# Second block's attention: three distances of the head planner and the spacing in the last group are changed

## Chip, core and metric

The kernel runs on one core of one Trainium2 chip. The metric is the device time of one execution in microseconds (us); the time of before is the median of three runs. Engines are called as the profile calls them: PE (TensorE, matmuls), DVE (VectorE), ACT (ScalarE), POOL (GpSimd) and SP (SyncE, which here only issues DMAs). PEld is PE's weight load.

## What is computed

Two transformer blocks follow each other on 256 tokens of width 2048, all in fp32. The first block (a gated delta rule, an RWKV scan, cross attention, an MLP) is not touched. The second block projects to q, k, v and a gate g for 32 heads of width 64. Sixteen heads (groups (0,0) and (0,1), eight heads each) mix three dilated windows, and sixteen (groups (1,0) and (1,1)) attend in a 2-D neighbourhood. Both come down to a softmax over at most 256 keys with a bias that also carries the mask:

```python
s = einsum('bhqd,bhkd->bhqk', q, k) * scale + bias
p = softmax(s)
o = einsum('bhqk,bhkd->bhqd', p, v)
y = concat(o) * silu(g)
out = layer_norm(ALPHA * x + y @ w_out)
```

## The kernel before

Each fp32 product is made of three matmuls over halves hi and lo: hi*hi, lo*hi, hi*lo. A weight matrix comes in pieces of 512 KB (`piece`, line 132): SP fetches `raw`, ACT rounds it to `whi` (line 106), DVE takes the rest, `wlo` = raw - whi (line 143). raw, whi and wlo have three buffers each. One piece feeds 12 matmuls of 128x512 (in `as_parts`, used for v) or 24 of 128x256 (in `ws_parts`, used for q, k and g). These matmuls write `acc` and are called big products below.

In the second block `main2` yields the big products of v, q and k for one group of eight heads, then for the next, and at last the gates of group (0,0) and (0,1). A group's heads are handed over when its k is complete; they run beside the big products that come next. So the heads of (0,0), (0,1) and (1,0) run beside v, q and k of the group after them, and those of (1,1) beside two gates. Heads are numbered 0 to 31 here in that order: 0 to 7 are the first group, 24 to 31 the last.

A head (`head`, from line 1374) has three places on PE, and yields twice between them:

- S, the scores: four matmuls into `s2p`. Then DVE adds the bias and takes the maximum (L1395, two of them, and L113), ACT takes the exponential with its sum (`s` on L106, two of them), DVE inverts the sum (L1401) and scales (L115, two of them).
- T, the transposition: four matmuls of `s` into `t2p` (L196). Then ACT rounds it to `ph`, and DVE takes the rest, `pl`.
- O, the output: four matmuls `o2p` from v, `ph` and `pl`. Then ACT and DVE add the two halves into `oall`.

PE's order is written by hand. `steps` keeps a count `now` that grows by 0.66 for each few big products and by the first number of a head's yield; the second number is how far `now` has to move on before the head's next place may be issued. `HEADS` (8.0) and `HEADS_END` (5.5, last group) are the distances between the starts of two heads, and the 7.0 in the loop is the distance between the end of a group's k and its first head. `main2` yields None before k of a group is written out, and then all heads that still run are finished first. DVE, ACT, POOL and SP are ordered by the tile framework's scheduler, which sees PE's order; `whi` and `wlo` have high priority there. Each engine works its own list in order. The PSUM buffers of s2p, t2p and o2p are four in one ring; `bias`, `s`, `ph` and `pl` have three buffers each. A head's bias is fetched by SP two heads ahead (`ta` for the first two groups, `tn` for the last two, where POOL adds a mask), and may start once L1395 of the head three before it is done. SP's list holds these fetches between the fetches of weights.

Of the kernel before, what the change touches and what calls it, by code (L numbers as in the profile page):

```python
# [19 lines left out]
ALPHA = 2.0 ** 0.25  # L20
C_DECAY = 0.5 * math.exp(-0.5)
INV_LAT = 42.0
HEADS, HEADS_END = 8.0, 5.5
WARM = 11
PART = 0.66

# [39 lines left out]
def block_kernel(tc, a, out, dbg=None, stop=99):  # L66
# [35 lines left out]
    def mm(o, l, r, start=True, stop=True):  # L102
        nc.tensor.matmul(o, l, r, start=start, stop=stop)  # L103

    def act(o, i, f=AF.Copy, **kw):
        return nc.scalar.activation(o, i, f, **kw)  # L106

    def tt(o, x, y, op, eng=None):
        (eng or nc.vector).tensor_tensor(out=o, in0=x, in1=y, op=op)  # L109

    def ts(o, x, s1, op0, s2=None, op1=None, eng=None):
        if op1 is None:
            (eng or nc.vector).tensor_scalar(out=o, in0=x, scalar1=s1, scalar2=None, op0=op0)  # L113
        else:
            (eng or nc.vector).tensor_scalar(out=o, in0=x, scalar1=s1, scalar2=s2, op0=op0, op1=op1)  # L115
# [6 lines left out]
    def pst(shape, name):  # L122
        return PS["pool"].tile(shape, F32, name=name, tag="ps", bufs=8 - PS["mm"])
# [70 lines left out]
    def tr(o, i):  # L194
        n = i.shape[0]
        nc.tensor.transpose(o, i, ident[0:n, 0:n])  # L196
# [45 lines left out]
    def split(src, h, l, scale=None):  # L242

        if scale is None:
            act(h, src)
            tt(l, src, h.bitcast(F32), SUB)
        else:
            act(h, src, scale=scale)
            stt(l, src, scale, h.bitcast(F32), MUL, SUB)
# [828 lines left out]
    now, need, ms = 0.0, None, main()  # L1078
    with tc.manual_schedule(engines={nc.tensor.engine}):
        while True:  # L1080
# [6 lines left out]
            if q is not None:  # L1087
                if stage[q][3] not in done:
                    stage[q][1] = now + 0.1
                    r = 0, 0.1  # L1090
                else:
                    r = next(stage[q][0], "end")
# [12 lines left out]
            if need is None and ms is not None:  # L1105
                r = next(ms, "end")
# [8 lines left out]
            else:  # L1115
                now = max(now, min(u[1] for u in stage if u and not u[2]))
# [180 lines left out]
    def at2(shape, name, bufs=1, dt=F32):  # L1297
        return atp.tile(shape, dt, name=name, tag=name, bufs=bufs)
# [78 lines left out]
    def head(key, i, bias):  # L1377

        c, e = divmod(i, 2)
        grp, hf = key  # L1380
        if not bias:
            bias[:] = [(bias_a, bias_b)[grp](8 * hf + j) for j in range(2)]
        q, (k, kl) = qk["q", c, key], qk["k", c, key]
        b = bias.pop(0)
        sp = pst([128, 2, T], "s2p")
        for t in range(2):
            tk = slice(t * 128, t * 128 + 128)
            mm(sp[:, t, :], q[:, e, tk], k[:, e, :], stop=False)
            mm(sp[:, t, :], q[:, e, tk], kl[:, e, :], start=False)
        if i + 2 < 8:  # L1390
            bias.append((bias_a, bias_b)[grp](8 * hf + i + 2))
        s = at2([128, 2, T], "s", bufs=3)
        mx = at2([128, 2], "mx2", bufs=3)
        for t in range(2):
            nc.vector.tensor_tensor_reduce(out=s[:, t, :], in0=sp[:, t, :], in1=b[:, t, :], scale=1.0,  # L1395
                                           scalar=-3e38, op0=ADD, op1=MAX, accum_out=mx[:, t:t + 1])
        ts(mx, mx, -1.0, MUL)
        rs = at2([128, 2], "rs2", bufs=3)
        for t in range(2):
            act(s[:, t, :], s[:, t, :], AF.Exp, bias=mx[:, t:t + 1], accum_out=rs[:, t:t + 1])  # L1400
        nc.vector.reciprocal(out=rs, in_=rs)  # L1401
        for t in range(2):
            ts(s[:, t, :], s[:, t, :], rs[:, t:t + 1], MUL, 0.5, MUL)
        yield 0.47, 5.5
        tp = pst([128, 2, T], "t2p")
        for t in range(2):
            for m in range(2):
                tr(tp[:, m, t * 128:(t + 1) * 128], s[:, t, m * 128:(m + 1) * 128])
        ph = at2([128, 2, T], "ph2", bufs=3, dt=F32R)
        pl = at2([128, 2, T], "pl2", bufs=3, dt=F32R)  # L1410
        split(tp, ph, pl)
        yield 0.44, 3.0

        op = pst([128, T], "o2p")
        for m in range(2):
            v = qk["v2", m, key][:, i]
            both = v.rearrange("p s d -> p (s d)")
            if m == 0:
                mm(op, both, ph[:, m, :], stop=False)
            mm(op[0:64, :], v[:, 0, :], pl[:, m, :], start=False, stop=False)  # L1420
            if m == 1:
                mm(op, both, ph[:, m, :], start=False)
        own = slice(64 * e, 64 * e + 64)
        o4 = qk["o", key]
        act(o4[own, c, :], op[0:64, :])
        tt(o4[own, c, :], op[64:128, :], o4[own, c, :], ADD)
        yield 0.71, 0
# [15 lines left out]
    def main2():  # L1443


        for key in ((0, 0), (0, 1), (1, 0), (1, 1)):
            o = 4096 * key[0] + 512 * key[1]

            def emit_v2(t, p, key=key):

                v = at2([128, 8, 2, 64], "v2", bufs=4, dt=F32R)
                split(p.rearrange("p (h d) -> p h d", h=8), v[:, :, 0, :], v[:, :, 1, :], rf[:, t:t + 1])
                qk["v2", t, key] = v

            def emit_q(c, p, key=key):
                emit_q2(c, p, key)

            def emit_k(c, p, key=key):
                emit_k2(c, p, key)
            yield from as_parts(w2, o + 2048, fh, fl, emit_v2)  # L1460
            yield from ws_parts(w2, [(o, 512, 0)], fh, fl, emit_q)
            yield from ws_parts(w2, [(o + 1024, 512, 0)], fh, fl, emit_k, needs=(None,))
            o4 = fix.tile([128, 4, T], F32, name="oall", tag="mix", bufs=4)
            oall.extend(o4[:, c, :] for c in range(4))
            qk["o", key] = o4
            bias = []
            yield [head(key, i, bias) for i in range(8)], HEADS if key != (1, 1) else HEADS_END
        yield from gate(0, 0)
        yield from gate(0, 1)
        yield None  # L1470

    now, begin, space, waiting, active = 0.0, 0.0, 0.0, [], []

    def steps(until):

        nonlocal now, begin
        while True:
            if waiting and begin <= until():
                active.append([now, waiting.pop(0)])
                begin = now + space  # L1480
            a = min((a for a in active if a[0] <= until()), key=lambda a: a[0], default=None)
            if a is None:
                return
            r = next(a[1], None)
            if r is None:
                active.remove(a)
            else:
                now = max(now, a[0]) + r[0]
                a[0] = now + r[1]

    with tc.manual_schedule(engines={nc.tensor.engine}):
        for r in main2():
            if r is None:
                steps(lambda: 1e9)
            elif isinstance(r, tuple):
                waiting.extend(r[0])
                begin, space = now + 7.0, r[1]
            else:
                now += r
                steps(lambda: now)  # L1500
# [88 lines left out]
```

## Time and profile before

| | us |
|---|---|
| median of three runs | 2265.58 (2262.42 to 2269.85) |
| the profiled execution | 2254.19 |
| its span on the core | 2252.3 |
| PE busy, of the span | 2192.2 (97%) |
| DVE busy | 1385.5 (62%) |
| ACT busy | 1115.4 (50%) |

The trace counts from the start of the span. The heads of the second block stand between 1792 and 2111. What lies ahead of that is the first block and the first v, q and k, and what lies behind it the last two gates, the output product and the layer norm. An instruction's row gives its start, its duration and, in brackets, how long its engine stood idle before it and what ended that. Matmuls are pipelined: the duration of one is longer than its distance to the next one. Rows of the chain of waits give a stretch's start, its length and what ran.

### The profile page before, as it was taken

To read this page: it belongs to the slowest core of one execution; us is meant where nothing else is said; L and a number is where in the kernel's file an instruction comes from. 1 tells how busy PE (TensorE), PEld (TensorE's weight loads), DVE (VectorE), ACT (ScalarE), POOL (GpSimd) and SP (SyncE) were. 2 spreads that over 40 slices of the span, in tenths; PEclk is the share of its full clock that TensorE was granted. 3 is DMA by queue.
4 is the path that set the end of the run, shared out by engine and by line. 5 is a ranking of instruction groups with operands and counts; after the bars stand their busy time and mean duration, and the time that the engine had idled before them with its cause. 6 is when DMAs were issued, how large, how long until landed. Compare 5 with 4: busy or idle time off the path is not lost.

```text
span 2252.3 us, 39057 instructions
## 1 busy us (share of the span) xinstructions
PE 2192.2 (97%) x15517; PEld 2012.9 (89%) x15517; DVE 1385.5 (62%) x2241; ACT 1115.4 (50%) x1799; POOL 263.7 (12%) x537
## 2 busy tenths in 40 slices
PE   9999999999999999999999999999999999998997
PEld 8998989889988899889998898898888988898986
DVE  6676677785644556555554455455556677777765
ACT  5455554553544545454444444344344556656542
POOL 0037255264200000000000000000000000121000
PEclk9999999999999999999999999999999999999999
DMA  6554344343466554456665665665656666565554
GB/s 215 185 162 125 104 141 140 116 144 117 150 215 212 185 173 150 153 187 186 188 190 192 194 189 190 195 188 190 193 187 221 184 177 181 173 173 162 193 191 146
DMA packets 229204, 391.77 MB, mean 174 GB/s; under 512 B 39902, under 2 KB 47836, under 8 KB 228765
## 3 DMA queue, kind: packets, MB, share of 16 engines
q1 hardware_dynamic: 227153, 385.37, 55.4%
q10 hardware_dynamic: 1324, 3.84, 0.5%
q8 instruction: 121, 1.98, 0.4%
q14 instruction: 62, 0.51, 0.1%
q0 software_dynamic: 544, 0.07, 0.0%
HBM read 386.25 MB, written 2.97 MB: 173 GB/s over the span
## 4 chain that ended last, share of the span: by engine, by line
PE 84%; POOL 6%; DVE 4%; issue 2%; DMA 2%; ACT 2%; SPq 0%; POOLq 0%; DVEq 0%; ACTq 0%
PE acc L103 76%; POOL Xt L109 3%; POOL X L109 2%; DVE wlo L143 1%; DMA nb<-scr 1%; ACT whi L106 1%; PE o2p L103 1%; PE t2p L196 1%; PE s2p L103 1%; PE tp L196 1%; DMA raw<-in_w_in_dram 1%; PE op L103 1%; PE xs L103 1%; PE xo L103 0%; DVE gv L118 0%
## 5 line engine op out<-in xcount | busy, mean ns | idle before, releaser
L143 DVE TENSOR_TENSOR wlo<-raw,whi 128x1024 fp32r<-128x1024 f32 (+1 forms) x696 | 852.5, 1226 | 723.9 <-ACT whi L106 719.6
L106 ACT ACTIVATE whi<-raw 128x1024 fp32r<-128x1024 f32 (+1 forms) x696 | 734.4, 1056 | 869.2 <-PE acc L103 743.4
L103 PE MATMUL acc<-ah,whi 128*128 128x256 f32 x3120 | 886.1, 284 | 2.3 <-ACT ah L106 1.6
L103 PE MATMUL acc<-al,whi 128*128 128x256 f32 x3120 | 873.7, 280 | 0.0
L103 PE MATMUL acc<-ah,wlo 128*128 128x256 f32 x3120 | 872.4, 280 | 0.7 <-DVE wlo L143 0.7
L103 PEld LDWEIGHTS acc<-ah,whi 128*128 128x128 f32 x3120 | 588.7, 189 | 7.3 <-issue 2.7
L103 PEld LDWEIGHTS acc<-al,whi 128*128 128x128 f32 x3120 | 588.8, 189 | 1.4 <-issue 0.9
L103 PEld LDWEIGHTS acc<-ah,wlo 128*128 128x128 f32 x3120 | 587.5, 189 | 1.1 <-DVE wlo L143 0.9
L103 PE MATMUL acc<-wlo,ah 128*128 128x512 f32 x704 | 275.3, 391 | 0.1
L103 PE MATMUL acc<-whi,al 128*128 128x512 f32 x704 | 275.0, 391 | 0.0
L103 PE MATMUL acc<-whi,ah 128*128 128x512 f32 x704 | 267.3, 396 | 0.0
L103 PE MATMUL acc<-wlo,uh 128*128 128x512 f32 x512 | 199.5, 390 | 0.0
L103 PE MATMUL acc<-whi,ul 128*128 128x512 f32 x512 | 199.2, 389 | 0.0
L103 PE MATMUL acc<-whi,uh 128*128 128x512 f32 x512 | 179.4, 389 | 0.0
L103 PEld LDWEIGHTS acc<-whi,al 128*128 128x128 f32 x704 | 132.7, 188 | 27.9
L103 PEld LDWEIGHTS acc<-wlo,ah 128*128 128x128 f32 x704 | 132.9, 189 | 26.4 <-DVE wlo L143 0.6
L103 PEld LDWEIGHTS acc<-whi,ah 128*128 128x128 f32 x704 | 132.7, 189 | 26.1 <-issue 0.3
L103 PEld LDWEIGHTS acc<-whi,ul 128*128 128x128 f32 x512 | 96.1, 188 | 20.0
L103 PEld LDWEIGHTS acc<-whi,uh 128*128 128x128 f32 x512 | 96.1, 188 | 19.8
L103 PEld LDWEIGHTS acc<-wlo,uh 128*128 128x128 f32 x512 | 96.1, 188 | 19.7
L109 POOL TENSOR_TENSOR Xt<-X,nb 128x60 f32<-128x60 f32 (+24 forms) x186 | 82.4, 443 | 171.6 <-DMA nb<-scr 152.9
L1363 POOL MEMSET klz<- 64x256 f32 x8 | 2.4, 306 | 696.1 <-PE acc L103 695.8
(522 smaller groups left out, 1852.4 us busy)
## 6 DMA issues: line engine op xcount, KB each, us to landing
raw<-in_w_in_dram SPq DMA_DIRECT2D x240, 512.0 KB
raw<-in_mlp_w_up_dram SPq DMA_DIRECT2D x128, 512.0 KB
raw<-in_mlp_w_down_dram SPq DMA_DIRECT2D x128, 512.0 KB
raw<-in_w_out_dram SPq DMA_DIRECT2D x64, 512.0 KB
raw<-in_xattn_wk_dram SPq DMA_DIRECT2D x32, 512.0 KB
raw<-in_xattn_wv_dram SPq DMA_DIRECT2D x32, 512.0 KB
raw<-in_xattn_wq_dram SPq DMA_DIRECT2D x32, 512.0 KB
raw<-in_xattn_wo_dram SPq DMA_DIRECT2D x32, 512.0 KB
```

What stands on the lines that cost most here:

```text
L103: nc.tensor.matmul(o, l, r, start=start, stop=stop)
L106: return nc.scalar.activation(o, i, f, **kw)
L109: (eng or nc.vector).tensor_tensor(out=o, in0=x, in1=y, op=op)
L143: last["dve"] = nc.vector.tensor_tensor(out=lo, in0=raw, in1=hi.bitcast(F32), op=SUB)
L196: nc.tensor.transpose(o, i, ident[0:n, 0:n])
L1363: nc.gpsimd.memset(kl[other, e, :].bitcast(F32), 0.0)
```

## The change

Four numbers change. A head's T may now come 9.0 instead of 5.5 counts behind its S, and its O 3.5 instead of 3.0 behind its T. A group's first head may begin 4.5 instead of 7.0 counts behind the end of its k. In the last group the heads start 5.0 instead of 5.5 counts apart.

```diff
-HEADS, HEADS_END = 8.0, 5.5
+HEADS, HEADS_END = 8.0, 5.0
...
             ts(s[:, t, :], s[:, t, :], rs[:, t:t + 1], MUL, 0.5, MUL)
-        yield 0.47, 5.5
+        yield 0.47, 9.0
         tp = pst([128, 2, T], "t2p")
...
         split(tp, ph, pl)
-        yield 0.44, 3.0
+        yield 0.44, 3.5
...
                 waiting.extend(r[0])
-                begin, space = now + 7.0, r[1]
+                begin, space = now + 4.5, r[1]
```

No instruction is added or removed on any engine. On PE the order of T and the next head's S is turned round. At the first two heads there stood before, from the first head's T on (`s_18843` is its s; `s2p_18914` are the second head's scores):

```order
L196 MATMUL t2p_18893<-cst_63,s_18843 128x128 x4
L103 MATMUL acc_18776<-whi_18904,ah_17327 128x512
L103 MATMUL acc_18776<-wlo_18905,ah_17327 128x512
L103 MATMUL acc_18776<-whi_18904,al_17328 128x512
L103 MATMUL acc_18776<-whi_18904,ah_17327 128x512
L103 MATMUL acc_18776<-wlo_18905,ah_17327 128x512
L103 MATMUL acc_18776<-whi_18904,al_17328 128x512
L103 MATMUL s2p_18914<-k2_18741,q2_18471 128x256
L103 MATMUL s2p_18914<-klz0_18061,q2_18471 128x256
```

And in the changed kernel, where `s_18825` is the first head's s and `s2p_18890` are the second head's scores:

```order
L103 MATMUL s2p_18890<-k2_18741,q2_18471 128x256
L103 MATMUL s2p_18890<-klz0_18061,q2_18471 128x256
L103 MATMUL s2p_18890<-k2_18741,q2_18471 128x256
L103 MATMUL s2p_18890<-klz0_18061,q2_18471 128x256
L103 MATMUL acc_18777<-whi_18877,ah_17327 128x512
L103 MATMUL acc_18777<-wlo_18878,ah_17327 128x512
L103 MATMUL acc_18777<-whi_18877,al_17328 128x512
L196 MATMUL t2p_18912<-cst_63,s_18825 128x128 x4
```

T has moved behind the next S. Counted in PE's whole order: between a head's S and its T stood 48 big products of 128x256 and the four matmuls of another head's O; now there are 72, with an O, a T and an S of other heads. At the first head of the first three groups it was 27 of 128x512, now 39 and an S; at head 24 it was 48 of 128x256 and an S, now 78 and an S. Between T and O it was 24 of 128x256 and an S, now 36 (at a group's first head 12 of 128x512 and an S, now 18). A group's first S stands 12 big products of 128x512 (24 of 128x256 at head 24) earlier. The distance between two heads of the last group comes out the same but for one.

DVE at the second group's first head (head 8; `klz` and `qky` belong to the writing out of k), before:

```order
L109 TENSOR_TENSOR klz3_18064<-qky_19747,k2_19749 64x256 x2
L143 TENSOR_TENSOR wlo_19859<-raw_19856,whi_19858 128x1024
L1395 ISA s_19824,mx2_19825<-s2p_19816,bias_19810 128x256
L1395 ISA mx2_19825 128x1
L1395 ISA s_19824,mx2_19825<-s2p_19816,bias_19810 128x256
L1395 ISA mx2_19825 128x1
L143 TENSOR_TENSOR wlo_19886<-raw_19883,whi_19885 128x1024
L113 TENSOR_SCALAR mx2_19825<-mx2_19825 128x2
L143 TENSOR_TENSOR wlo_19930<-raw_19927,whi_19929 128x1024
L1401 RECIPROCAL rs2_19829<-rs2_19829 128x2
L115 TENSOR_SCALAR s_19824<-s_19824,rs2_19829 128x256 x2
```

The same place in the changed kernel:

```order
L143 TENSOR_TENSOR wlo_19841<-raw_19838,whi_19840 128x1024
L109 TENSOR_TENSOR klz2_18063<-qky_19738,k2_19740 64x256
L1395 ISA s_19806,mx2_19807<-s2p_19798,bias_19792 128x256
L1395 ISA mx2_19807 128x1
L1395 ISA s_19806,mx2_19807<-s2p_19798,bias_19792 128x256
L1395 ISA mx2_19807 128x1
L109 TENSOR_TENSOR klz2_18063<-qky_19738,k2_19740 64x256
L109 TENSOR_TENSOR klz3_18064<-qky_19747,k2_19749 64x256 x2
L113 TENSOR_SCALAR mx2_19807<-mx2_19807 128x2
L143 TENSOR_TENSOR wlo_19859<-raw_19856,whi_19858 128x1024
L1401 RECIPROCAL rs2_19811<-rs2_19811 128x2
L115 TENSOR_SCALAR s_19806<-s_19806,rs2_19811 128x256 x2
```

L1395 has moved ahead of one `wlo` and of the last `klz`, and one `wlo` instead of two stands between L1395 and L115. SP at the same place, before (`raw_19945` is the eighth and last piece of v's weights, `bias_19900` the bias of head 11):

```order
L138 DMA raw_19883<-in_w_in_2_dram 128x2x512
L138 DMA raw_19927<-in_w_in_2_dram 128x2x512
L138 DMA raw_19945<-in_w_in_2_dram 128x2x512
L1327 DMA bias_19900<-ta_9228 128x256 x2
L138 DMA raw_19999<-in_w_in_2_dram 128x2x512
```

And in the changed kernel:

```order
L138 DMA raw_19902<-in_w_in_2_dram 128x2x512
L138 DMA raw_19920<-in_w_in_2_dram 128x2x512
L1327 DMA bias_19876<-ta_9228 128x256 x2
L138 DMA raw_19945<-in_w_in_2_dram 128x2x512
L138 DMA raw_19999<-in_w_in_2_dram 128x2x512
```

The bias has moved ahead of the last piece of v. At the first group's first head it stood so already. ACT's list there has `whi` of the three last pieces of v, then the second head's exponentials, then the first head's `ph`; before it had one `whi` less there and no exponential of the second head.

DVE in the last group at head 26, before (`rs2_22038` and `s_22033` are head 26, `o2p_22089` is head 25, `s2p_22102` head 27):

```order
L1401 RECIPROCAL rs2_22038<-rs2_22038 128x2
L109 TENSOR_TENSOR oall_21750<-o2p_22089,oall_21750 64x256
L1395 ISA s_22114,mx2_22115<-s2p_22102,bias_21939 128x256
L1395 ISA mx2_22115 128x1
L1395 ISA s_22114,mx2_22115<-s2p_22102,bias_21939 128x256
L1395 ISA mx2_22115 128x1
L115 TENSOR_SCALAR s_22033<-s_22033,rs2_22038 128x256
```

In the changed kernel (`rs2_22001` and `s_21996` are head 26, `o2p_22037` is head 24, `t2p_22050` head 25, `s2p_22065` head 27):

```order
L1401 RECIPROCAL rs2_22001<-rs2_22001 128x2
L109 TENSOR_TENSOR oall_21750<-o2p_22037,oall_21750 64x256
L115 TENSOR_SCALAR s_21996<-s_21996,rs2_22001 128x256 x2
L109 TENSOR_TENSOR pl2_22056<-t2p_22050,ph2_22055 128x512
L1395 ISA s_22077,mx2_22078<-s2p_22065,bias_21903 128x256
```

L115 of head 26 no longer stands behind L1395 of head 27, and `pl` of head 25 stands behind L115 of head 26. Over all heads, `pl` stands behind the next head's L115 at 13 of them; before it did at 3.

## Rows read from the trace of the kernel before

**Rows 1.** The page: busy us of each engine, share of the span, instructions

```profile
PE 2192.2 (97%) x15517; PEld 2012.9 (89%) x15517; DVE 1385.5 (62%) x2241; ACT 1115.4 (50%) x1799; POOL 263.7 (12%) x537
```

**Rows 2.** PE's waits, group by group: us in total, times, longest

```profile
PE t2p L196 <- DVE s L115: 1.8, 1, 1.8
...
PE o2p L103 <- DVE pl L109: 1.0, 1, 1.0
...
PE t2p L196 <- DVE s L115: 4.8, 2, 2.7
...
PE t2p L196 <- DVE s L115: 4.6, 2, 2.4
...
PE t2p L196 <- DVE s L115: 8.3, 7, 2.7
```

**Rows 3.** Stretches at the lower clock: busy us per engine, granted clock, DMA

```profile
1805.40:1808.80 3.40, 3.38 (x10) 2.80 (x11) 3.07 (x10) 1.36 (x5) 0.00 (x0) 0.50 0.73 192
...
2054.60:2058.00 3.40, 3.40 (x18) 3.40 (x17) 2.34 (x5) 2.40 (x6) 0.73 (x1) 0.50 0.82 232
```

**Rows 4.** Second and last group: length, busy PE, PEld, DVE, ACT, POOL, clock

```profile
1876.50:1959.70 83.20, 78.36 (x578) 73.87 (x578) 62.48 (x131) 51.08 (x99) 6.04 (x6) 1.00 0.61 178
...
2044.30:2111.00 66.70, 58.42 (x462) 56.75 (x462) 51.93 (x124) 37.02 (x79) 8.32 (x10) 0.95 0.49 142
```

**Rows 5.** Chain of waits: big products without a gap, 128x256 and 128x512

```profile
1851.46 4.21 PE acc L103 x36
...
1889.86 4.11 PE acc L103 x18
```

**Rows 6.** Head 8 in order of time, PE and DVE: from S to T

```profile
1876.90 0.28 PE L103 MATMUL s2p<-klz,q 128*128 128x256 f32 x1
...
1885.51 0.63 PE L196 MATMUL t2p<-cst,s 128*128 128x128 f32 x4 [2.17 <-DVE s L115]
...
1880.07 0.42 DVE L1395 CUSTOM_DVE_ANT_0 s<-s2p,bias 128x256 f32<-128x256 f32 x1
...
1885.01 0.62 DVE L115 TENSOR_SCALAR s<-s,rs 128x256 f32<-128x256 f32 x2
```

**Rows 7.** Chain of waits at head 24: its S and its L115

```profile
2044.51 0.46 PE s2p L103 x4
...
2053.26 1.01 DVE s L115 x2
```

**Rows 8.** Head 0 in order of time, SP, ACT and PE: from T to O

```profile
1794.60 0.81 SPq L1327 DMA_DIRECT2D bias<-ta  x2
1796.14 3.79 SPq L138 DMA_DIRECT2D raw<-in_w_in_dram  x3
...
1802.45 1.06 ACT L106 ACTIVATE whi<-raw 128x1024 fp32r<-128x1024 f32 x1 [4.18 <-DMA raw<-in_w_in_dram]
1803.41 0.58 ACT L106 ACTIVATE ph<-t2p 128x512 fp32r<-128x512 f32 x1
...
1804.05 0.39 PE L103 MATMUL o2p<-ph,v 128*128 128x256 f32 x1 [1.25 <-ACT ph L106]
```

**Rows 9.** DVE's groups of instructions, last group, then L115 of the second

```profile
L143 DVE TENSOR_TENSOR wlo<-raw,whi 128x1024 fp32r<-128x1024 f32 x17 | 20.8, 1225 | 11.8 <-ACT whi L106 11.7
L115 DVE TENSOR_SCALAR s<-s,rs 128x256 f32<-128x256 f32 x16 | 6.9, 468 | 0.2
...
L115 DVE TENSOR_SCALAR s<-s,rs 128x256 f32<-128x256 f32 x16 | 4.9, 349 | 0.2
```

**Rows 10.** A usual head (head 10) in order of time: S's last, L115, T, `pl`

```profile
1895.99 0.28 PE L103 MATMUL s2p<-klz,q 128*128 128x256 f32 x1
...
1899.90 0.61 DVE L115 TENSOR_SCALAR s<-s,rs 128x256 f32<-128x256 f32 x2
...
1902.19 0.60 PE L196 MATMUL t2p<-cst,s 128*128 128x128 f32 x4
...
1904.67 0.69 DVE L109 TENSOR_TENSOR pl<-t2p,ph 128x512 fp32r<-128x512 f32 x1
```

## The prediction

> **What bounds the kernel now.** I read the page first: PE is busy for 97% of the span [rows 1], so only PE's own time counts, and time is to be had only where PE stands still or runs slower than it could. Then PE's waits, in four windows that each begin with a group's first S [rows 2]. Nearly all of them are of one kind: T waits for L115, 1.8 us in the first group, 4.8 in the second, 4.6 in the third, 8.3 in the last; together 19.5 us. Besides, head 0's O waits 1.25 us for `ph` [rows 8] and 1.0 us for `pl`. That is 21.8 us. Third, the granted clock: there are four stretches of 3.4 us in the heads' part at 0.50, which is 1.2 of 2.4 GHz; two are shown [rows 3], the others begin at 1969.3 and 2085.3. Each begins within about 2 us of the end of such a wait. A stretch of 3.4 us at half speed costs 1.7 us, four cost 6.8 us. So what the heads cost PE beyond work is 21.8 + 6.8 = 28.6 us, 1.3% of the execution. That is the most that the change can win, since it removes no work.
>
> **Why T waits.** Prices of PE: 128x256 products run at 4.21 / 36 = 0.117 us each, 128x512 at 4.11 / 18 = 0.228 us [rows 5]; the four matmuls of an S take 0.46 us [rows 7], and I use that for a T or an O too. Between S and T there stand 48 x 0.117 + 0.46 = 6.1 us before (27 x 0.228 = 6.2 us at a group's first head). A usual head needs less: head 10's S ended at 1896.27, its L115 at 1900.51, 4.2 us, and its T came at 1902.19 without a wait [rows 10]. But at head 8 L115 ended 8.45 us behind S (1877.18 to 1885.63), and T waited 2.17 us [rows 6]; at head 24 it took 9.3 us (2044.97 to 2054.27) [rows 7]. These are the two kinds of place that wait: a group's first heads, where k is still written out and the `wlo` of the next pieces stand ahead on DVE, and heads beside the writing out of q or gates. I found no chain longer than that of head 24.
>
> **T moved back, first three groups.** The new distance is 72 x 0.117 + 3 x 0.46 = 9.8 us, at a group's first head 39 x 0.228 + 0.46 = 9.35 us. That is beyond 8.45 and, at the heads that are not first, beyond everything seen. The chain of head 8 should even get shorter, since one `wlo` of 1.2 us has left it. What hides the longer distance are big products that PE has to do anyway, and they run out nowhere: the last O of a group stands at the end of k as before. I take all the waits of T there as gone: 1.8 + 4.8 + 4.6 = 11.2 us. The bounds: nothing of it if L115 slides back as far as T, all of it as taken.
>
> **The earlier start.** A group's first S moves 12 x 0.228 = 2.7 us forward. It needs k and `klz` of the first two heads only, and the order has those written out ahead of it; I cost it at nothing. What moves with it is the bias of the fourth head, on SP. At head 0 the bias stood ahead of the last piece of v already: that piece, the first of the fetches from 1796.14, came only at 1802.4, ACT sat idle for 4.18 us, `ph` stood behind it, and O waited [rows 8]. This piece now stands behind a bias in all four groups, and the next head's exponentials stand between it and `ph`. Against that, O comes later: at head 0 it would have been due at 1804.05 - 1.25 = 1802.8, and is now due 2.7 us earlier by S, 3.2 us later by T and 18 x 0.228 - (12 x 0.228 + 0.46) = 0.9 us later by O, so at 1804.2. `ph` was ready at 1804.0 then. The bounds are no wait at all and 2.3 us in each group, 9.2 us. I take 2.0 us for all four together, nearer to none, because the bias itself now goes out earlier too; against 2.3 us before that is a gain of 0.3 us.
>
> **The last group.** Here distance alone doesn't do it. At head 24 it is 78 x 0.117 + 0.46 = 9.6 us against the 9.3 needed. But DVE is busy for 51.93 us of the group's 66.7 us [rows 4]; without PE's waits and its two slow stretches the group is 66.7 - 8.3 - 3.4 = 55.0 us long, and DVE would be busy for 94% of it. The tightest place by the order is head 29's T. From head 24's S to it PE has 258 big products and 17 steps of heads, 258 x 0.117 + 17 x 0.46 = 38.0 us. From L1395 of head 24 to L115 of head 29 DVE has 91 instructions; at the group's mean, 51.93 / 124 = 0.419 us, that is 38.1 us. It can begin only some 3.6 us behind S: 3.3 us before (2.9 us behind S's end at head 8 [rows 6], and S itself), 2.8 us more because S is earlier, 2.5 us less for a `wlo` and three `klz` that no longer stand ahead. So DVE is 38.1 + 3.6 - 38.0 = 3.7 us late, and PE waits that long. Of 8.3 us I take 4.6 us as won. The bounds: all 8.3 if DVE's instructions overlap as tightly as they can, nothing if its own idle time comes back. Before, it stood idle 11.7 us for `whi` here [rows 9]; as far as `whi` in its turn waits for PE to free a buffer, that goes with PE's waits. The start distance 5.0 instead of 5.5 moves nearly nothing: the heads still stand 5.6 us apart in PE's order.
>
> **The clock.** The two slow stretches of the first three groups follow head 0's O and head 16's T; with those waits mostly gone I take both as gone, and one of the two in the last group: 3 x 1.7 = 5.1 us. Bounds: 0 and 6.8.
>
> **The sum.** 11.2 + 0.3 + 4.6 + 5.1 = 21.2 us. From the profiled execution's 2254.19 us that leaves 2233.0 us, a ratio of 0.9906. The median of the runs shown is 2265.58, 0.5% above the profiled execution, so I take the ratio from there: 2244.3 us.
>
> **Rivals.**
>
> *The last piece of v behind a bias.* O of each group's first head waits as at head 0. For it: the order on SP, and 4.18 us of idle ACT where it stood so before. Against it: before, only one group had it, the DMAs have room (share 0.61 in the second group [rows 4]), and O is due later. It costs 9.2 - 2.3 = 6.9 us where I took a gain of 0.3, and three slow stretches instead of one: 11.2 - 6.9 + 4.6 + 1.7 = 10.6 us won, 2254.9 us.
>
> *DVE becomes the bound of the last group.* Its waits stay at 8.3 us and both slow stretches with them: 11.2 + 0.3 + 3.4 = 14.9 us won, 2250.6 us. For it: 94%, and POOL's adding of the mask, 8.32 us in ten instructions there [rows 4], beside which L115 takes 468 ns instead of 349 [rows 9], 1.9 us over sixteen. The Trainium skill, page "SBUF — State Buffer", section "SBUF: two separate sides", says that a VectorE instruction with two SBUF inputs and a GpSimd instruction exclude each other for the whole instruction. By that rule up to 8.32 us could be lost rather than 1.9, DVE would need 51.93 + 6.4 = 58.3 us of 55.0, and this rival would be certain; the trace shows a quarter of it.
>
> *The wait moves to O, and the kernel gets slower.* `pl` of a head now stands behind L115 of the next head on DVE in 13 places. Before, `pl` ended 2.6 us behind T's end (1902.79 to 1905.36 [rows 10]), and the new distance from T to O is 36 x 0.117 = 4.2 us. Where the order is the new one, the next S stands some 1.6 us ahead of T, its L115 comes 4.2 us behind it and `pl` 0.7 us later, about 3 us behind T: 1.2 us to spare. A chain like head 8's, 4.2 us longer than that of head 10, uses that up and 3.0 us more. If all 13 did so, that would be 13 x 3.0 = 39 us lost against 21.8 us of waits won, with the clock as before: 17 us more, 2282.8 us. The kernel is slower than before from 21.8 / 13 = 1.7 us a place on. Against it: chains of 8 us and more were few before, nine waits or so of 32, and one `wlo` less stands in head 8's.
>
> *The change doesn't do what it says.* DVE's and ACT's order follow PE's; if L115 moves back with T, the waits stay: about 2264 us. The rows of the order at head 8 speak against it.
>
> **How the numbers follow.** Chances: forecast 0.56, piece of v 0.18, DVE bound 0.16, wait at O 0.04, nothing gained 0.06. A measurement of this kernel can tell about 0.3%, 6.8 us, from no change. The first three all lie beyond it, less a little for each: faster 0.85, same 0.09, slower 0.06. The range reaches from nearly all 28.6 us won, and a spread of the runs of a few us, 2232 us, to beyond the first two rivals, 2259 us; what is left out are the last two rivals and the tails.
>
> **What would show it.** In the changed kernel's profile: no wait of PE for L115 before the last group's first S; in the last group some 4 us, at heads 28 to 30; waits of o2p at the groups' first heads of some 2 us in all, with ACT idle on a fetch of weights before; one or two stretches at half clock instead of four; DVE above 85% busy in the last group. Wrong would be: waits of o2p for `pl` at many heads (third rival), or T still waiting at heads 8, 13, 16 and 21, where L115 would then end more than 9.4 us behind S.

## The result, and the profile after

The changed kernel takes 2234.56 us (median of four runs, 2230.97 to 2237.7), the kernel before took 2264.0 in the same comparison (four runs, 2252.67 to 2269.85). The ratio is 0.9875, interval 0.9834 to 0.9917: about 28 us, 1.25%, faster. The forecast was a ratio of 0.9906 and 2244.3 us.

The profiled execution took 2237.7 us, its span 2235.8, only 16.5 us less than before, because its first block, which is the same in both, ran slower: up to the same place in PE's work the profile of before had needed 1789.6 us (first S at 1792.3, less the 2.7 that it stood later), this one needed 1799.15. One stretch at half clock there is 13.7 us long and has no counterpart before; all of them ahead of the first S come to 34 us, before to 17. Rows of the windows give start and end, length, busy us of PE, PEld, DVE, ACT and POOL with their instructions, the granted clock, the DMA share and GB/s; these are three stretches of the changed kernel:

```profile
399.50:413.20 13.70, 13.42 (x103) 9.74 (x102) 7.55 (x21) 3.92 (x13) 2.73 (x8) 0.50 0.12 39
...
539.60:1799.10 1259.50, 1259.00 (x8211) 1145.94 (x8210) 697.57 (x844) 593.24 (x807) 22.42 (x48) 1.00 0.59 186
1799.10:2225.00 425.90, 419.05 (x2956) 390.76 (x2955) 321.69 (x626) 247.04 (x443) 30.50 (x33) 1.00 0.63 186
```

The third row is the stretch that the change concerns: from the first S up to the kernel's tail (the layer norm, at 0.50 from 2225.6 on, before from 2242.3) the granted clock is 1.00 throughout, where [rows 3] showed two of four stretches at 0.50. So I compare the part from the first S to the end. It took 462.7 us before (2252.3 - 1789.6) and takes 436.7 now (2235.8 - 1799.15): 26.0 us less. PE's waits there, for the first, the second and the last group of heads and the gates behind them (the third group has none; us in total, times, longest):

```profile
PE o2p L103 <- DVE pl L109: 0.7, 1, 0.7
...
PE o2p L103 <- DVE pl L109: 0.2, 1, 0.2
...
PE o2p L103 <- DVE pl L109: 1.3, 2, 1.1
...
PE acc L103 <- DVE wlo L143: 0.5, 1, 0.5
PE acc L103 <- ACT whi L106: 0.3, 1, 0.3
```

Against [rows 2] every wait of T for L115 is gone, 19.5 us, in the last group too. PE is nearly always busy in the four groups, and DVE in the last one for 51.28 of 56.0 us, 92%, where [rows 4] had 51.93 of 66.7 (the rows are the second, the third and the last group):

```profile
1878.10:1956.60 78.50, 78.31 (x578) 73.98 (x577) 62.50 (x131) 51.48 (x99) 5.67 (x6) 1.00 0.66 189
1956.60:2035.00 78.40, 78.33 (x598) 74.91 (x597) 63.47 (x131) 51.51 (x99) 15.64 (x16) 1.00 0.65 189
2035.00:2091.00 56.00, 54.72 (x468) 54.31 (x467) 51.28 (x124) 38.85 (x84) 8.26 (x10) 1.00 0.58 166
```

Head 8 in order of time, PE's and DVE's rows, to be read beside [rows 6]: S begins at 1878.17, L115 ends at 1885.36, 6.5 us behind the end of S (8.45 before, since one `wlo` less stands between), and T comes at 1888.02 without a wait:

```profile
1878.53 0.28 PE L103 MATMUL s2p<-klz,q 128*128 128x256 f32 x1
...
1888.02 0.60 PE L196 MATMUL t2p<-cst,s 128*128 128x128 f32 x4
...
1883.40 1.23 DVE L143 TENSOR_TENSOR wlo<-raw,whi 128x1024 fp32r<-128x1024 f32 x1 [0.65 <-ACT whi L106]
...
1884.74 0.62 DVE L115 TENSOR_SCALAR s<-s,rs 128x256 f32<-128x256 f32 x2
```

The waits that are left in the four groups are all O's for `pl`, and the longest is that of head 26. Its `ph` was done at 2058.68; its `pl` stood on DVE behind a `wlo`, two steps of a gate and L1395 of head 28:

```profile
2062.08 0.45 PE L103 MATMUL o2p<-pl,v 128*64 128x256 f32 x2 [1.10 <-DVE pl L109]
...
2060.99 0.42 DVE L1395 CUSTOM_DVE_ANT_0 s<-s2p,bias 128x256 f32<-128x256 f32 x1
...
2061.34 0.69 DVE L109 TENSOR_TENSOR pl<-t2p,ph 128x512 fp32r<-128x512 f32 x1
...
2058.10 0.58 ACT L106 ACTIVATE ph<-t2p 128x512 fp32r<-128x512 f32 x1
```

### The profile page after: what moved, and what is told of

The parts are those of the page before. It is cut to its first block, busy times and chain, and to the rows that moved or that the text cites. A ratio compares the mean times of both kernels' runs of the same rounds, so it can differ in the third digit from the quotient of the medians.

```text
span 2235.8 us, 39039 instructions
## 1 busy us (share of the span) xinstructions
PE 2192.9 (98%) x15517; PEld 2013.8 (90%) x15517; DVE 1387.7 (62%) x2241; ACT 1117.5 (50%) x1799; POOL 259.3 (12%) x537
## 4 chain that ended last, share of the span: by engine, by line
PE 82%; DVE 6%; POOL 4%; DMA 3%; ACT 2%; issue 2%; SPq 0%; POOLq 0%; ACTq 0%; DVEq 0%
PE acc L103 75%; POOL X L109 2%; DVE wlo L143 2%; POOL Xt L109 2%; DMA raw<-in_w_in_dram 1%; DMA nb<-scr 1%; ACT whi L106 1%; PE o2p L103 1%; PE tp L196 1%; PE xs L103 1%; PE xo L103 0%; PE s2p L103 0%; PE op L103 0%; PE t2p L196 0%; DVE gv L118 0%
## 5 line engine op out<-in xcount | busy, mean ns | idle before, releaser
L109 POOL TENSOR_TENSOR Xt<-X,nb 128x60 f32<-128x60 f32 (+24 forms) x186 | 68.8, 370 | 175.3 <-DMA nb<-scr 161.5
```

## The experiments

The part ahead of the first S moves by up to 13 us from profile to profile, counted to the same place in PE's work. So the single profiles are compared by **lost time**: PE's idle time from the first S up to the tail, plus half of the length of the stretches at half clock there. It was 28.6 us before and is 3.1 in the changed kernel. Taken off the part from the first S on (and with the start of the groups counted as 4.5 in all), it leaves 431 to 435 us in every kernel below, so it holds what differs.

| kernel | T, O, start, spacing | T waits, us | O waits, us | at half clock | lost, us | ratio (interval) |
|---|---|---|---|---|---|---|
| before | 5.5, 3.0, 7.0, 5.5 | 19.5 | 2.3 | 13.6 us | 28.6 | |
| before, again | the same | 17.9 | 3.1 | 10.2 us | 26.1 | |
| changed | 9.0, 3.5, 4.5, 5.0 | 0 | 2.2 | 0 | 3.1 | 0.9875 (0.9834 to 0.9917) |
| T alone | **9.0**, 3.0, 7.0, 5.5 | 0 | 6.7 | 3.4 us | 8.3 | 0.9934 (0.9913 to 0.9956) |
| start alone | 5.5, 3.0, **4.5**, 5.5 | 11.7 | 0.3 | 6.8 us | 15.7 | 0.9959 (0.994 to 0.9978) |
| start 2.0 alone | 5.5, 3.0, **2.0**, 5.5 | 20.8 | 0 | 20.4 us | 31.2 | one run |
| changed, old start | 9.0, 3.5, **7.0**, 5.0 | 0.3 | 3.3 | 3.4 us | 5.7 | 0.9915 (0.9885 to 0.9945) |
| changed, old O | 9.0, **3.0**, 4.5, 5.0 | 0 | 2.9 | 0 | 3.1 | 0.9891 (0.9858 to 0.9924) |
| changed, old spacing | 9.0, 3.5, 4.5, **5.5** | 0 | 1.5 | 0 | 2.1 | one run |
| changed, T 7.25 | **7.25**, 3.5, 4.5, 5.0 | 2.3 | 3.8 | 3.4 us | 7.9 | one run |
| changed, T 12 | **12.0**, 3.5, 4.5, 5.0 | 0 | 16.4 | 20.4 us | 26.9 | one run |
| changed, spacing 3.5 | 9.0, 3.5, 4.5, **3.5** | 1.9 | 0.6 | 0 | 2.6 | one run |
| changed, less mask | as changed | 0 | 0.6 | 0 | 0.6 | one run |
| changed, start 2.0 | 9.0, 3.5, **2.0**, 5.0 | 0 | 0.2 | 0 | 0.2 | 0.9848 (0.9819 to 0.9877) |

A ratio compares a kernel with the kernel before on the same chip. The waits and the lost time are of one profile each; the second row shows how far one kernel's move. Waits of PE for other things than T and O, and gaps under 0.15 us, stand in the lost time alone, up to 0.9 us.

**T alone.**

```diff
-        yield 0.47, 5.5
+        yield 0.47, 9.0
```

> Only T is moved back (9.0 counts behind S); O, the groups' start and the last group's spacing are as before. In PE's order T now stands 9.7 us of products behind S instead of 5.9. Quantity: time from head 0's first S to the end of the span, 460.0 us in the profile of before and 436.7 - 2.7 = 433.9 us of the same work in the changed kernel; PE's waits of T, 19.5 us before. Theory (the distance from S to T does nearly all of it): waits of T 0 to 2 us, no or one stretch at half clock, 434 to 438 us, so 22 to 26 us of the 26 won. Rival A (the earlier start is what shortens the chain at a group's first heads, and they need it): T still waits at heads 0, 8, 16, 24 and the heads behind them, some 1 to 2 us each, 445 to 450 us. Rival B (pl needs O's new distance too): waits of O for pl of 0.5 us and more at many heads, 5 to 10 us in all.

It took 440.8 us from the first S to the end, which is 19.2 won, against the 22 to 26 of the theory. The waits:

```profile
PE o2p L103 <- DVE pl L109: 4.9, 11, 0.8
PE o2p L103 <- ACT ph L106: 1.8, 1, 1.8
```

This one number takes away every wait of T, so rival A is out. But 6.7 us of waits of O are left, 2.3 of them at head 0, so it is not all of the change. Rival B is there in part: `pl` is waited for 11 times, 4.9 us in all, but for 0.5 us and more at three places only.

The edit does more than move T away, since DVE's order follows PE's. At heads 8, 16 and 24 the chain from S to L115 is 5.0, 5.0 and 4.8 us here, where it was 8.45, 8.45 and 9.3 before; a T at the old distance would hardly have waited for it. This is head 8, whose S ended at 1884.38:

```profile
1886.48 0.42 DVE L1395 CUSTOM_DVE_ANT_0 s<-s2p,bias 128x256 f32<-128x256 f32 x1
...
1887.36 1.23 DVE L143 TENSOR_TENSOR wlo<-raw,whi 128x1024 fp32r<-128x1024 f32 x1
...
1888.81 0.61 DVE L115 TENSOR_SCALAR s<-s,rs 128x256 f32<-128x256 f32 x2
```

The distance itself is what covers the chains of heads 5, 13 and 21 (7.3, 7.8 and 7.9 us) and of heads 27 to 29 (8.0 to 10.0 us). That it covers a long chain at a first head too is shown further down, with a start of 2.0.

**The start alone, and an earlier one.** First 4.5:

```diff
-                begin, space = now + 7.0, r[1]
+                begin, space = now + 4.5, r[1]
```

> Only the groups' start is moved (4.5 counts instead of 7.0 behind the end of k); T, O and the spacing are as before. T stands 5.9 us of products behind S as in the kernel before. Theory (distance does it): T's waits stay at 16 to 21 us, three to five stretches at half clock, and from the first S to the end 460.0 + 2.7 = 463 us, within 3 us. Rival A (the earlier start shortens the chain of a group's first heads, since a wlo less stands in it): T's waits at heads 0, 8, 16 and 24 shrink by 1.2 us each, and with the heads behind them 5 to 10 us go.

Here the theory fell and the rival held in the main: 451.0 us, 11.7 won, 7.8 us of T's waits gone, with T nowhere further from S. At head 8 one `wlo` stands between L1395 and L115, the chain is 6.6 us instead of 8.45, and T waits 0.34 us instead of 2.17:

```profile
1879.55 0.41 DVE L1395 CUSTOM_DVE_ANT_0 s<-s2p,bias 128x256 f32<-128x256 f32 x1
...
1882.18 1.23 DVE L143 TENSOR_TENSOR wlo<-raw,whi 128x1024 fp32r<-128x1024 f32 x1 [0.64 <-ACT whi L106]
...
1883.51 0.62 DVE L115 TENSOR_SCALAR s<-s,rs 128x256 f32<-128x256 f32 x2
...
1884.01 0.63 PE L196 MATMUL t2p<-cst,s 128*128 128x128 f32 x4 [0.34 <-DVE s L115]
```

Is it the earlier start that helps, or the place that the scheduler happens to give `wlo`? The same edit with 2.0 instead of 4.5 tells that:

> The kernel before with the groups' start at 2.0 counts behind the end of k; T, O and the spacing as before. With 4.5 counts alone T's waits had fallen from 19.5 to 11.7 us, which the theory of the distance had not expected. Theory now: that gain came from one wlo less between L1395 and L115 at a group's first head and at heads behind it, an accident of the order; with 2.0 counts two wlo stand there again, so T waits 1.2 to 2.3 us at heads 0, 8 and 16 again (0.3 us with 4.5 counts), and lost time (PE's waits from the first S on plus half of the stretches at half clock) is 20 to 28 us, against 15.7 with 4.5 and 28.6 before. Rival (an earlier start is better in itself, since bias, k and q are there and DVE is less loaded then): T waits 0.5 us or less at the first heads, lost time 10 to 16 us.

The earlier start loses everything again, 31.2 us, three more than the theory's range allows, and the rival is out. Two `wlo` stand in head 8's chain, and it is 8.6 us long:

```profile
1887.25 0.42 DVE L1395 CUSTOM_DVE_ANT_0 s<-s2p,bias 128x256 f32<-128x256 f32 x1
...
1887.97 1.23 DVE L143 TENSOR_TENSOR wlo<-raw,whi 128x1024 fp32r<-128x1024 f32 x1
...
1892.42 1.23 DVE L143 TENSOR_TENSOR wlo<-raw,whi 128x1024 fp32r<-128x1024 f32 x1 [1.10 <-ACT whi L106]
...
1893.75 0.62 DVE L115 TENSOR_SCALAR s<-s,rs 128x256 f32<-128x256 f32 x2
...
1894.25 1.09 PE L196 MATMUL t2p<-cst,s 128*128 128x128 f32 x4 [2.39 <-DVE s L115]
```

With T close behind S, what a start is worth was decided by the order on DVE, and that turned with the start: two `wlo` in head 8's chain at 7.0, one at 4.5, two at 2.0.

**The changed kernel without its start.**

```diff
-                begin, space = now + 4.5, r[1]
+                begin, space = now + 7.0, r[1]
```

> The changed kernel with the groups' start put back to 7.0. T 9.7 us of products behind S, O 4.1 us behind T. Theory: nothing is missed, since nothing waited for the start: from the first S to the end 433.9 us (the 436.7 of the changed kernel less 2.7 for the start), within 2 us; waits of T none before the last group. Rival A (the start matters): T waits again at first heads, 4 us and more in all. Rival C (the earlier start costs by the bias in front of the last piece of v): waits of O at heads 0, 8 and 16 get smaller than the 0.7 us of the changed kernel, by at most that.

From the first S to the end 437.6 us, 3.7 above the theory, which so fell; there is no wait of T but 0.3 us in the last group. What came back are waits of O: 1.65 us at head 0 (1.07 for `ph` and 0.58 for `pl`), with a stretch at half clock behind them, and 0.34 us at each of heads 7, 15 and 23. This is head 15's:

```profile
1948.68 0.38 PE L103 MATMUL o2p<-ph,v 128*128 128x256 f32 x1
1949.40 0.46 PE L103 MATMUL o2p<-pl,v 128*64 128x256 f32 x2 [0.34 <-DVE pl L109]
```

Its T had stood at 1947.4 with next to nothing between: the end of k finishes all heads that still run. The longer distance uses up the room there, and the earlier start gives it back (3.3 us between T and O in the changed kernel, 0.7 here). T alone, which also starts at 7.0, has the same three waits of 0.34 us. At head 0 the rival with the bias ahead of v's last piece ran the other way: the earlier start made that wait smaller, 0.74 for 1.65 us. T alone has 2.3 us there, and no kernel with T at 9.0 and a start of 4.5 has more than 0.74.

**O and the spacing.** Each is put back alone.

```diff
-        yield 0.44, 3.5
+        yield 0.44, 3.0
```

> The changed kernel with O put back to 3.0 counts behind T: 3.4 us of products between T and O instead of 4.1, 3.2 in the last group instead of 3.9. Theory: pl ends about 3 us behind T where it stands behind the next head's L115, so most places keep their cover and the waits of O grow from 3 us to at most 6, mainly in the last group; 437 to 441 us from the first S to the end (436.7 in the changed kernel). Rival B (O's distance is needed in all 13 places where pl stands behind the next L115): O waits at ten places or more, 0.7 us each, 7 us and more in all, with half-clock stretches behind some of them.

436.6 us and 3.1 lost (O waits 0.7 us longer, and the wait of 0.8 us at `acc` doesn't come): with the other three in place the new distance of O is worth nothing that shows. With the old start it may be worth something: T alone loses 8.3 us, the changed kernel with its old start 5.7, and these two differ in O and in the spacing of the last group.

```diff
-HEADS, HEADS_END = 8.0, 5.0
+HEADS, HEADS_END = 8.0, 5.5
```

> The changed kernel with the heads of the last group 5.5 counts apart again instead of 5.0; in PE's order only the second head of the group moves, by 0.7 us. Theory: worth nothing, the waits of the last group 1 to 2 us and lost time (PE's waits from the first S on plus half of the stretches at half clock) within 1 us of 3.1. Rival (the spacing relieves or loads DVE): waits of the last group 4 us and more, as was forecast for the change.

2.1 us lost, 1.1 of it in the last group: as expected, worth nothing that shows.

**T at 7.25 and at 12.0.**

```diff
-        yield 0.47, 9.0
+        yield 0.47, 7.25
```

> The changed kernel with T 7.25 counts behind S instead of 9.0: 7.3 us of products between S and T (7.4 to 7.9 at first heads and in the last group) instead of 9.7. Lost time here means PE's waits from the first S on plus half of the stretches at half clock: 28.6 us in the kernel before, 3.1 in the changed one. Theory (T waits where the chain from S to L115 is longer than the distance): in the changed kernel the chains above 7.3 us were those of heads 14 (8.2), 22 (8.1), 28 (10.1), 29 (9.9) and 30 (7.6); T waits 0.5 to 3 us at these and hardly elsewhere, 3 to 6 us in all, and lost time comes to 5 to 10 us. Rival (what counts is that T stands behind the next S, not how far): no waits of T, lost time 4 us or less.

Lost time came as expected, 7.9 us, but not where it was expected: T waits at head 28 alone, less than the theory's 3 to 6 us, and O for `pl` at heads 5, 13 and 21:

```profile
PE o2p L103 <- DVE pl L109: 3.8, 3, 1.5
PE t2p L196 <- DVE s L115: 2.3, 1, 2.3
```

The chains at heads 14 and 22 are again the long ones, 9.2 and 9.4 us. There DVE is writing out q, and `pl` of the head ahead stands in the same jam; its O comes first and holds PE, so that T finds its L115 done. The third rival of the prediction is real at these places, 1.0 to 1.5 us each, not 3.0.

```diff
-        yield 0.47, 9.0
+        yield 0.47, 12.0
```

> The changed kernel with T 12.0 counts behind S: 12.2 to 12.7 us of products between them instead of 9.7. Theory (9.7 us already covers all but the last group's longest chains of 10 us): no waits of T, lost time (PE's waits from the first S on plus half of the stretches at half clock) 1 to 4 us, against 3.1 with 9.0 counts. Rival (three buffers of s and four of s2p, t2p and o2p hold S back when two or three heads overlap): S or L1395 waits for a buffer, lost time 6 us or more.

Both fell: 26.9 us lost, but no wait of T, and none for a buffer that the profile shows. Most of it is at the last heads of the first three groups, 4.6 to 4.8 us each, with a stretch at half clock that begins in each. At head 7 T stood at 1870.48, in the middle of k's writing out, and `ph` came behind eight writes of `k` on ACT:

```profile
1871.52 3.45 ACT L106 ACTIVATE k<-qky 64x256 fp32r<-64x256 f32 x8
1874.87 0.57 ACT L106 ACTIVATE ph<-t2p 128x512 fp32r<-128x512 f32 x1
...
1875.50 0.58 PE L103 MATMUL o2p<-ph,v 128*128 128x256 f32 x1 [4.42 <-ACT ph L106]
```

So distance is bounded from both sides: by the chain of S to L115, and by the end of k.

**Closer heads in the last group.**

```diff
-HEADS, HEADS_END = 8.0, 5.0
+HEADS, HEADS_END = 8.0, 3.5
```

> The changed kernel with the heads of the last group 3.5 counts apart instead of 5.0: 3.6 to 3.9 us of products between two heads' S instead of 5.6, T and O as far behind as before. Theory (DVE is next to become the bound there: a head costs DVE 3.1 us, and 3.7 us of products bring 1.3 pieces of wlo, 1.6 us, together 4.7 of 3.7 us): PE comes to wait in the last group, 4 to 9 us of T and O waits, growing from head to head, lost time 6 to 14 us (3.1 in the changed kernel). Rival (DVE's 92% is only work that moves aside; there is room): lost time 4 us or less and O31 earlier by nothing.

The theory fell: 2.6 us lost. DVE's work does pile up (the chain is 7.0 us at head 24 and 12.0 at head 31), but T stands 9 to 10 us behind S, and the group is nearly over before the pile is larger than that: T waits at heads 30 and 31 only, 0.9 us each. The windows are the stretch of the eight S with 2 us behind it, and 56 us as for the changed kernel:

```profile
2033.20:2062.00 28.80, 28.73 (x246) 28.34 (x245) 27.47 (x79) 23.07 (x56) 10.43 (x10) 1.00 0.64 176
2033.20:2089.20 56.00, 54.06 (x458) 53.07 (x456) 48.12 (x122) 38.12 (x82) 10.43 (x10) 1.00 0.64 194
```

DVE is at 95% in the first one, and PE stands still for 0.1 us of it.

**POOL beside DVE.**

```diff
-            tt(b[:, t, :], b[:, t, :], namask, ADD, eng=nc.gpsimd)
+            tt(b[:, t, 0:16], b[:, t, 0:16], namask[:, 0:16], ADD, eng=nc.gpsimd)
```

> The changed kernel in which POOL adds the mask to 16 of the 256 keys of a head's bias only, so 240 keys of the last two groups go without mask; everything else stands as it is. POOL's ten adds of the last group were 838 ns each, 8.3 us; DVE was busy 51.3 us of 56.0 there and O waited 1.3 us for pl. Theory (POOL's adding hardly takes anything from DVE, since L115 took 349 ns in the changed kernel with the same POOL work): DVE's busy time falls by less than 1 us, waits of the last group stay within 0.5 us of 1.3. Rival (POOL and DVE shut each other out while POOL adds): DVE's busy time in the last group falls by 2 to 8 us and the waits there go to none.

The theory fell: waits in the last group go from 1.3 us to none, and lost time to 0.6. In the second, the third and the last group:

```profile
1880.85:1958.87 78.02, 78.02 (x577) 73.94 (x576) 60.95 (x131) 51.16 (x99) 2.31 (x6) 1.00 0.68 190
1958.87:2036.98 78.11, 78.11 (x598) 74.90 (x597) 61.11 (x131) 51.23 (x99) 7.91 (x16) 1.00 0.67 190
2036.98:2093.00 56.02, 56.02 (x481) 55.84 (x480) 50.62 (x127) 39.74 (x86) 5.30 (x10) 1.00 0.59 167
```

In the second group POOL is 3.4 us less busy than in the changed kernel and DVE 1.5 us less, over the same 131 instructions; in the third POOL 7.7 us and DVE 2.4, again over 131. In the last group three instructions more fall into the window; like by like it is some 2.4 us for POOL's 3.0. What stretches there is not L115 (in the second and third group it is, with 381 and 374 ns for 351 and 350). It is L113, 0.9 us of the 2.4 (the group of the changed kernel, then of this one), and for the other 1.5 us `wlo` and two steps of the gates, which read two tensors in SBUF each:

```profile
L113 DVE TENSOR_SCALAR mx<-mx 128x2 f32<-128x2 f32 x8 | 2.2, 279 | 0.1
```

```profile
L113 DVE TENSOR_SCALAR mx<-mx 128x2 f32<-128x2 f32 x8 | 1.3, 166 | 0.1
```

**The changed kernel with a start of 2.0.**

```diff
-                begin, space = now + 4.5, r[1]
+                begin, space = now + 2.0, r[1]
```

> The changed kernel with the groups' start at 2.0 instead of 4.5 counts behind the end of k. With T at its old distance the same step had taken lost time (PE's waits from the first S on plus half of the stretches at half clock) from 15.7 to 31.2 us, since two wlo stand between L1395 and L115 at heads 0, 8, 16 and 24. Theory (the longer distance covers such a chain, whatever the order makes of it): the chain from S to L115 is 8 us and more at these heads again, T stands 9.3 us behind S, no T waits before the last group and lost time is 2 to 5 us; 434 to 437 us from the first S to the end plus 2.7 us of start, 437 to 440 us. Rival (the start and the order of wlo are worth as much with the long distance): T waits 1 us or more at two of the four first heads, lost time 8 us or more.

The chains of heads 0, 8, 16 and 24 are 8.6, 8.1, 8.6 and 9.0 us, two `wlo` stand in them, and T, 9.2 us and more behind S, waits nowhere. This is head 8, whose S ended at 1875.37:

```profile
1876.36 0.42 DVE L1395 CUSTOM_DVE_ANT_0 s<-s2p,bias 128x256 f32<-128x256 f32 x1
...
1878.78 1.23 DVE L143 TENSOR_TENSOR wlo<-raw,whi 128x1024 fp32r<-128x1024 f32 x1 [0.32 <-ACT whi L106]
...
1881.48 1.23 DVE L143 TENSOR_TENSOR wlo<-raw,whi 128x1024 fp32r<-128x1024 f32 x1 [0.70 <-ACT whi L106]
...
1882.82 0.62 DVE L115 TENSOR_SCALAR s<-s,rs 128x256 f32<-128x256 f32 x2
...
1884.57 0.60 PE L196 MATMUL t2p<-cst,s 128*128 128x128 f32 x4
```

And this is the only wait from the first S on:

```profile
PE o2p L103 <- DVE pl L109: 0.2, 1, 0.2
```

The start moves S by nine big products here, 2.1 us, not by the 2.7 of the expectation; so counted, the part from the first S on is 433.4 us, 3.3 less than in the changed kernel, of which 2.9 us are lost time. It beats the kernel before, 0.9848 (0.9819 to 0.9877); against the changed kernel the intervals overlap, so the whole time doesn't separate the two. The theory held in its mechanism, and less was lost than the 2 to 5 us that it named.

**Before, again.**

> The kernel before once more, for the spread of one profile. Theory: waits are set by the order and repeat within 1 us (21.8 us from the first S on); stretches at half clock need not, so lost time is 25 to 32 us (28.6 before); the time up to the first S differs by up to 10 us, since the first block's half-clock stretches come and go. Rival (the first profile was an unusual one): waits of 17 us or less or 27 us or more.

PE stood idle for 21.0 us from the first S on (21.8 in the first profile), and 26.1 us were lost. Lost time of one kernel so moves by some 2.5 us from profile to profile, 1.7 us of it by the half-clock stretches. A difference of that size between two single profiles in the table shows nothing by itself.

## Why the prediction was right, and where it was off

The forecast left 28.6 - 21.2 = 7.4 us of lost time, 3.1 were measured: 2.4 less in the last group, 1.0 less at O, 1.7 less by the clock, and 0.8 more at `acc`, which the forecast didn't have.

- **T in the first three groups, 11.2 us.** Right, all gone, and shown by T alone. At the first heads the distance had less to cover than the step took: the chain of head 8 fell to 6.5 us, as the step half expected, and with the start alone, where it is 6.6 us, T waits 0.34 us at the old distance.
- **The earlier start, nothing.** Wrong as a price. Alone it was worth 13 us. Beside the other three numbers it is 2.6 us of lost time (5.7 to 3.1), about what one kernel moves by; but the waits at heads 0, 7, 15 and 23, 2.7 us in all, and the stretch at half clock behind the first are in both kernels with T at 9.0 and the old start (3.4 us in T alone), and 0.7 us of them in the changed one. The step looked at what the earlier S needs and not at what the later T and O use up at the other end of the group; "they run out nowhere" holds for PE's products, but not for the room ahead of the end of k, which the start of 4.5 keeps and T at 12.0 uses up.
- **O at the first heads, 2.0 us left.** 0.74 at head 0, none at heads 8, 16 and 24; 0.19 and 0.07 at heads 13 and 21 for `pl`. The bias ahead of the last piece of v made no wait at the other first heads. At head 0 ACT stood idle for 3.62 us on a fetch, with `ph` behind it; O was due late enough for `ph`, as the step had it, and waited 0.74 us for `pl`.
- **The last group, 3.7 us left.** Mis-sized. It was to be seen as T's waits at heads 28 to 30; it is 1.3 us, and O's, at heads 26 and 28. The working let DVE begin 3.6 us behind S; it began 2.1 behind (S24 at 2035.04, L1395 at 2037.16). L115 of head 29 ended at 2074.9, 37.7 us later, where 38.1 were taken. So DVE is 2.1 + 37.7 - 38.0 = 1.8 us late instead of 3.7; O's waits ahead of it had taken 1.3 of that, and PE's own work 0.4 more than the 38.0.
- **The clock, 5.1 us.** 6.8, all that there was: no wait above 1.1 us was left, and no stretch came.
- **DVE as the bound of the last group.** It didn't come about, at 92% busy and, with closer heads, not at 95%: a long distance from S to T lets DVE fall behind and catch up in the gates. But the part of POOL was undersized. I took a quarter of POOL's time, 1.9 us, from L115, which in the last group of the changed kernel was no slower than elsewhere (349 ns, [rows 9] had 468). The cost was there all the same, in other instructions: 1.5 us of DVE for 3.4 of POOL in the second group, 2.4 for 7.7 in the third, 2.4 for 3.0 in the last, so between three tenths and four fifths. I had quoted the exclusion for the whole instruction from the Trainium skill, page "SBUF — State Buffer", section "SBUF: two separate sides". The trace agrees as far as the kind goes, since most of what stretched reads two tensors in SBUF (1.5 of 2.4 us in the last group); DVE lost less than all of POOL's time.
- **The wait moves to O.** Only in small, but all that is left in the four groups is of this kind: 2.2 us of O for `pl` against 1.0 before, 0.26 us of it where `pl` stands beside the writing out of q (heads 13 and 21). At T 7.25 it is 3.8 us.
- **Nothing gained.** L115 didn't slide with T.

So the sum was 4 us short and right in its main term. What the long distance does is best seen in the two starts of 2.0: a like jam on DVE, with two `wlo` in the chains of the first heads, costs 31.2 us with T at 5.5 and 0.2 with T at 9.0. These two kernels differ in O and in the last spacing as well, each of which was worth nothing that shows when put back alone.

## What to carry to other kernels

Where a product waits for a chain through two other in-order engines, look first at the distance in the waiting engine's order: it covers the longest chain, whichever way a scheduler happens to order the two. Measure the longest chain and set the distance to about its length (here 9.7 us for chains of up to 10), no more: the same distance takes room from the next hard stop (here the end of k), so move the start forward as well. Expect the edit to change the other engines' order too, and measure the chains again. Judge such an edit by the waits and the stretches at half clock in its own part of the trace where an untouched part moves by 10 us from profile to profile.

## What the hardware showed that I had not expected

- **Half clock follows a wait of PE, but not every one.** In these fourteen profiles each stretch at 0.50 behind the first S and ahead of the kernel's tail began in a wait of 1.65 us or more (at one place, or two close together at one O) or within 1.6 us of its end; none occurred in the six kernels whose waits stayed at 1.1 us or less. But waits of 2.67 and 2.40 us (heads 13 and 21 of before) had none behind them, so a wait's length alone doesn't decide. What else does stays open.
- **A small add on POOL costs much of a large one.** In the last group 128x16 took 534 ns a piece, 128x256 838 ns; in the second group it was 391 and 952 ns.
- **POOL's adding seems to reach PE.** With the short adds O's waits for `pl` fell from 2.2 to 0.6 us. Lost time fell by 2.5 us, but 0.8 us of that is the wait at `acc`, which is also missing in a kernel with the whole adds (changed, old O). Each side is one profile.
